# Cosine-similarity attention: a third chunk of exponentials off ScalarE, wide casts of V, late Q sums on TensorE

## The chip, the cores and the metric

The kernel runs on one core of a Trainium2 chip. The core has a matrix engine (TensorE, "PE" in the profile, its weight loads "PEld"), VectorE ("DVE"), ScalarE ("ACT"), GpSimd ("POOL"), SyncE ("SP"), which here issues nearly all transfers, and 16 DMA engines. Each engine works through its own list of instructions in order and waits on semaphores for the others. TensorE writes to PSUM, from which VectorE and ScalarE read; GpSimd works on SBUF alone. The metric is the time of one execution on the device in microseconds (us); the time of a kernel is the median over its runs.

## The reference

Eight batches of twelve heads, 512 rows of 64 numbers each:

```
Q_norm = Q / (norm(Q, axis=-1) + 1e-10)          # Q, K, V: 8 x 12 x 512 x 64, float32
K_norm = K / (norm(K, axis=-1) + 1e-10)
scores  = einsum('bhqd,bhkd->bhqk', Q_norm, K_norm) / tau          # tau = 0.1
weights = exp(scores - max(scores)); weights /= sum(weights) + 1e-10
out     = einsum('bhqk,bhkd->bhqd', weights, V)
```

The scores lie between -10 and 10, so the kernel leaves out the subtraction of the maximum; it gets the row sums from a column of ones beside V.

## The kernel before

The 96 heads are worked as 48 pairs (s = 0 to 47). Each pair of heads goes through these steps, each of them one or a few "operations" of the program; names in brackets are the keys in the code, lines are those of the profile.

- Loads of Q, K and V by SyncE (LD, LV).
- Squares of Q and K on GpSimd in one instruction (SQ, L337), rounded to bf16.
- Their sums by row. For most K (and for Q of the first pairs), TensorE first adds eight slices of eight columns with eight matmuls against the identity (SSQ, L354, into a spare part of the bank for results), and VectorE reduces the rest (RED, L361, 128x64). Where TensorE takes no part, VectorE reduces all 128x512 squares (RED, L365). `on_pe(s, w)` decides which: `Q_ON_PE`, `BY_VECTOR`.
- An inverse square root for a group of pairs by some small VectorE steps (NEW, L389 to L398).
- Scaling of Q (VectorE) and of K (GpSimd, or VectorE for the pairs in `K_ON_DVE`) by it (SCL, L420).
- Eight transposes on TensorE into one PSUM bank (TR, L426, tile tps) and a copy of that bank by VectorE (EVA, L434, tile qt).
- Scores: for each of four chunks c of 128 keys, two matmuls of 512 columns, one for each head (SCO, L508, tile scps). This is called a score group. scps holds two of them, so a score group waits for the exponential two chunks earlier.
- The exponential of the chunk for both heads in one ScalarE instruction, 128x1024 (EXP, L531, tile et).
- A cast of V to bf16 on GpSimd (VC, L536, tile vb).
- Values: for each head h and each quarter i of the queries four matmuls of 65 columns (PV, L548), 32 in all for a pair, into one result bank for each head (tile ops).
- A reciprocal of the row sums (RCP, L559) and the multiplication by it (NRM, L561) on VectorE, here called the division; then the store by SyncE (ST, L565). The first values of the next pair in a bank wait for the division of the pair before.

For chunk 3 of pairs 37 and 45 (`OFF`) ScalarE takes no part: `poly` makes the exponential from a polynomial. TensorE puts that chunk's scores head by head into the bank of the transposes (SCX, L468), VectorE reads each twice (X, L473 and L475), GpSimd does four steps (Y 0 to 3, L479 and L480) and VectorE two more (Y 4 and 5, L486 and L480). Until VectorE has read the second head's scores, the transposes of the next pair wait.

The last pair ends in three pieces (`PIECES`: head 0; head 1 first half; head 1 second half), each with values (L576), reciprocal (L587), division (L589) and store (L593) of its own, by `last`.

No scheduler runs: `ORDER` is a list written out for each engine, of places in the list of operations, and each engine emits them in that order (negative entries are filler matmuls that keep TensorE busy at the start). `due` values decide nothing but which result bank the sums of which pair go to. `RINGS` gives the number of buffers: for Q and K (and vb), V, squares, scaled Q/K, transposed Q/K, exponentials, results and norms.

## Time and profile before

| | |
|---|---|
| time, median of three runs | 189.43 us (189.35 to 189.87) |
| the profiled execution's own time | 189.84 us |
| its span, from the first to the last instruction | 187.9 us |
| ACT busy | 180.8 us (96%), of it L531 174.3 |
| PE, and PEld, busy | 173.7 us (92%), 108.7 us (58%) |
| DVE busy | 172.3 us (92%) |
| POOL busy | 166.8 us (89%) |
| granted TensorE clock | 1.0 all through |
| DMA | 50.76 MB, 270 GB/s over the span |

Busy time is the union of an engine's instructions. Instructions of VectorE, ScalarE and TensorE overlap at their ends, so an instruction's own duration is longer than its distance to the next: an exponential of 128x1024 lasts 1163 ns in the mean, and the next one ends some 917 ns after it. [...]

Rows of the groups that the change touches, as count, mean duration and shape: L337 on GpSimd 44 x 1893 ns (128x1024); L420 on GpSimd 36 x 1042 ns and on VectorE 58 x 677 ns (128x512); L536 on GpSimd 48, most at 626 ns (128x512); L365 on VectorE 48 x 683 ns; L361 on VectorE 40 x 213 ns; L354 on TensorE 368 matmuls; L473 and L475 on VectorE 4 x 688 and 4 x 684 ns; L479 and L480 on GpSimd 4 x 1044 and 4 x 1892 ns; L486 and L480 on VectorE 2 x 1247 and 2 x 676 ns.

### The profile page before, as it was taken

The numbers are of one execution on the slowest core, as the hardware profiler recorded it, in microseconds if no ns is written. First come the engines' busy times: TensorE is split into PE (matmuls) and PEld (weight loads), VectorE is DVE, ScalarE is ACT, GpSimd is POOL, SyncE is SP. The second block draws the span as 40 slices with busy tenths as digits, with TensorE's granted clock in tenths as the row PEclk, the third lists the DMA queues.
The fourth block names the chain that finished last, engine by engine and source line by source line (L and its number), as shares of the span: only waits on it lengthen the run. The fifth ranks groups of instructions, "written<-read, shape, count | busy, mean of one in ns | idle before, by whom it ended". The sixth has DMA issues, their size and how long they took to land.

```text
span 187.9 us, 6635 instructions
## 1 busy us (share of the span) xinstructions
PE 173.7 (92%) x2694; PEld 108.7 (58%) x2694; DVE 172.3 (92%) x546; ACT 180.8 (96%) x212; POOL 166.8 (89%) x152
## 2 busy tenths in 40 slices
PE   6999999999998999999999999899999989999983
PEld 2655666566665666666666556556645446655552
DVE  2789999999999999999999999999999999988864
ACT  4799999999999999999999999999999999999992
POOL 4797999999999999999999999999999999696600
PEclk9999999999999999999999999999999999999999
DMA  4999999899999988999999999976996551312215
GB/s 148 356 350 349 348 354 331 233 328 370 379 385 375 326 243 264 333 304 297 361 379 381 380 380 301 306 244 198 302 336 194 173 167 59 112 59 76 95 59 169
DMA packets 52446, 50.76 MB, mean 270 GB/s; under 512 B 3136, under 2 KB 52416, under 8 KB 52416
## 3 DMA queue, kind: packets, MB, share of 16 engines
q1 hardware_dynamic: 51984, 50.02, 81.1%
q8 instruction: 21, 0.34, 0.8%
q10 hardware_dynamic: 432, 0.33, 0.5%
q14 instruction: 9, 0.07, 0.1%
HBM read 37.75 MB, written 12.58 MB: 268 GB/s over the span
## 4 chain that ended last, share of the span: by engine, by line
ACT 92%; PE 4%; DMA 1%; DVE 1%; issue 1%; POOL 0%
ACT et L531 90%; DMA qk<-in_Q_dram 1%; PE ops L548 1%; PE scps L508 1%; DVE xs L245 0%; PE ops L576 0%; ACT ys L379 0%; DVE ob L589 0%; PE scps L268 0%; POOL qn L258 0%; ACT nps L382 0%; PE tps L268 0%; ACT sq L239 0%; ACT et L522 0%; PE scps L194 0%
## 5 line engine op out<-in xcount | busy, mean ns | idle before, releaser
L531 ACT ACTIVATE et<-scps 128x1024 bf16<-128x1024 f32 (+1 forms) x191 | 174.3, 1151 | 0.5 <-PE scps L508 0.5
L337 POOL TENSOR_TENSOR sq<-qk 128x1024 bf16<-128x1024 f32 x44 | 82.7, 1893 | 1.4 <-DMA qk<-in_K_dram 1.2
L508 PE MATMUL scps<-qt 64*128 64x512 bf16 x380 | 75.2, 386 | 7.8 <-ACT et L531 4.4
L548 PE MATMUL ops<-vb,et 128*128 128x65 bf16 x1504 | 71.6, 194 | 1.1 <-DVE qn L420 0.5
L548 PEld LDWEIGHTS ops<-vb,et 128*128 128x128 bf16 x1504 | 55.1, 98 | 27.1 <-issue 17.4
L420 POOL TENSOR_TENSOR qn<-qk,rk 128x512 bf16<-128x512 f32 x36 | 37.2, 1042 | 2.8 <-DVE rk L394 2.5
L561 DVE TENSOR_TENSOR ob<-ops,rd 128x256 f32<-128x256 f32 x94 | 38.9, 417 | 0.4
L420 DVE TENSOR_TENSOR qn<-qk,nps 128x512 bf16<-128x512 f32 x58 | 38.5, 677 | 0.4 <-ACT nps L382 0.4
L434 DVE COPY qt<-tps 128x1024 bf16<-128x1024 bf16 x47 | 32.3, 687 | 2.6 <-PE tps L426 2.1
L426 PE MATMUL tps<-ident,qn 128*128 128x128 bf16 x376 | 33.9, 221 | 0.1
L508 PEld LDWEIGHTS scps<-qt 64*128 64x128 bf16 x380 | 18.9, 92 | 26.0 <-ACT et L531 11.8
L365 DVE TENSOR_REDUCE nps<-sq 128x8 f32<-128x512 bf16 x48 | 32.3, 683 | 0.0
L536 POOL TENSOR_SCALAR vb<-vf 128x512 bf16<-128x512 f32 x48 | 30.8, 655 | 0.2
L426 PEld LDWEIGHTS tps<-ident,qn 128*128 128x128 bf16 x376 | 21.4, 98 | 12.9 <-issue 6.6
L559 DVE RECIPROCAL rd<-ops 128x4 f32<-128x4 f32 x94 | 16.2, 176 | 3.3 <-PE ops L548 2.3
L354 PE MATMUL ops<-sq,ident 128*128 128x64 bf16 x368 | 18.5, 194 | 0.0
L354 PEld LDWEIGHTS ops<-sq,ident 128*128 128x128 bf16 x368 | 13.9, 98 | 4.1 <-issue 2.7
L361 DVE TENSOR_REDUCE nps<-ops 128x8 f32<-128x64 f32 x40 | 8.5, 213 | 0.6 <-PE ops L354 0.5
L389 DVE TENSOR_TENSOR nps<-nps,ys 128x32 f32<-128x32 f32 (+1 forms) x30 | 6.3, 209 | 0.1
L390 DVE SCALAR_TENSOR_TENSOR nps<-nps,ys 128x32 f32<-128x32 f32 (+1 forms) x30 | 6.2, 208 | 0.1
L480 POOL TENSOR_TENSOR xz<-xz 128x1024 f32<-128x1024 f32 x2 | 3.8, 1892 | 1.5 <-DVE xz L475 1.5
L191 PE MATMUL ops<-warm_in,ident 128*128 128x512 bf16 x8 | 3.6, 628 | 1.4 <-POOL ident L181 1.4
(61 smaller groups left out, 65.0 us busy)
## 6 DMA issues: line engine op xcount, KB each, us to landing
vf<-in_V_dram SPq DMA_DIRECT2D x48, 256.0 KB, 5.8
qk<-in_Q_dram SPq DMA_DIRECT2D x47, 256.0 KB, 5.0
qk<-in_K_dram SPq DMA_DIRECT2D x47, 256.0 KB, 5.7
out_dram<-ob SPq DMA_DIRECT2D x47, 256.0 KB, 3.9
qk<-in_Q_dram SPq DMA_DIRECT2D x2, 128.0 KB, 2.7
qk<-in_K_dram ACTq DMA_DIRECT2D x2, 128.0 KB, 2.9
out_dram<-ob SPq DMA_DIRECT2D x1, 128.0 KB, 1.7
out_dram<-ob ACTq DMA_DIRECT2D x1, 64.0 KB, 1.6
```

Of the source, the lines that this page charges most:

```text
L337: lambda e: e.tensor_tensor(out=sqf, in0=data, in1=data, op=ALU.mult))
L354: last = e.matmul(out=o_ps[bank][:, 320:384], lhsT=ident[:, :], rhs=sq[iqs][:, 8 * w : 8 * w + 8, 8 * k : 8 * k + 8], start=(k == 0), stop ...
L365: lambda e, w=w, dst=dst: e.tensor_reduce(out=dst, in_=sq[iqs][:, 8 * w : 8 * w + 8, :], axis=AX.X, op=ALU.add))
L420: lambda e, w=w, r=r: e.tensor_tensor(out=qn[iqn][:, w].rearrange("p t h d -> p h t d"), in0=qk[iq][:, w].rearrange("p h (t d) -> p h t d" ...
L426: last = e.transpose(t_ps[:, w, t, :], qn[iqn][:, w, t].rearrange("p h d -> p (h d)"), ident[:, :])
L434: lambda e: e.tensor_copy(out=qt[iqt][:, :, :, :].rearrange("p w t x -> p (w t x)"), in_=t_ps[:, :, :, :].rearrange("p w t x -> p (w t x)")))
L508: last = e.matmul(out=sc_ps[:, 2 * b + h, :], lhsT=qt[iqt][64 * h : 64 * h + 64, 1, c, :], rhs=qt[iqt][64 * h : 64 * h + 64, 0, :, :], sta ...
L531: lambda e, c=c, b=b, hs=hs: e.activation(out=et[iet][:, c, hs[0] : hs[-1] + 1, :], in_=sc_ps[:, 2 * b + hs[0] : 2 * b + hs[-1] + 1, :], f ...
L536: lambda e: e.tensor_scalar(out=vb[:, iq, :, :, 0:DIM].rearrange("p c h d -> p h c d"), in0=vf[iv][:, :, :].rearrange("p h (c d) -> p h c ...
L548: last = e.matmul(out=o_ps[h][:, 65 * t : 65 * t + 65], lhsT=et[iet][:, c, h, 128 * t : 128 * t + 128], rhs=vb[:, iq, c, h, :], start=(c = ...
L559: lambda e, h=h, grid=grid: e.reciprocal(out=rd[io][:, h, :], in_=grid[:, :, DIM]))
L561: lambda e, h=h, grid=grid: e.tensor_tensor(out=ob[io][:, h], in0=grid[:, :, 0:DIM], in1=rd[io][:, h, :].unsqueeze(2).to_broadcast([128, N ...
```

## The change

- `OFF` gets chunk 3 of pair 31; ScalarE has 186 exponentials of 128x1024 in its list instead of 187.
- V is cast for two pairs in one instruction of 128x1024 (`JOINT` with "v", from pairs 8 and 9 on; 20 wide casts and 8 narrow ones for 48 narrow ones). The arrays of Q/K, V and vb become one tensor each, and vb's order of heads and chunks is swapped, so that two pairs lie in one access.
- `Q_ON_PE` holds pairs 24 to 46, so that their Q squares are summed first by TensorE.
- `K_ON_DVE` gets pairs 23, 24, 26, 28, 30 and 32.
- Pairs 45, 37 and 31 (`BY_CHUNK`) run their values chunk by chunk, with the polynomial's chunk last, instead of query quarter by query quarter. `LATER` lets the values of pairs 37 and 31 take their turn in the result banks a pair later.
- `RINGS`: 16 buffers for Q and K instead of 15, 6 for scaled Q/K instead of 4, 6 for results instead of 8.
- `ORDER` is another list on every engine. Branches for joint scaling and joint division are there, but `JOINT` names none of them.

```diff
+    def join(self, name, members, eng, kind, due, needs, emit, *rest):
+
+        op = self.add((name, members[-1]) + rest, eng, kind, due, needs, emit)
+        for s in members[:-1]:
+            self.ops[(name, s) + rest] = op
...
-    vb = sb("vb", [128, R_QK, NT, 2, DIM + 1], bf16)
+    vb = sb("vb", [128, R_QK, 2, NT, DIM + 1], bf16)
...
-    for s, w in sorted(((s, w) for s in range(NP) for w in range(2) if on_pe(s, w)), key=lambda j: (due_red(j[0]), j)):
+    for s, w in sorted(((s, w) for s in range(NP) for w in range(2) if on_pe(s, w)), key=lambda j: (j[0] >= EARLY and not j[1], due_red(j[0]), j)):
...
-    for s in range(NP):
+    for s in sorted(range(NP), key=lambda i: i + (1.5 if i in LATER else 0)):
         for h in range(2):
             bank_free[s, h] = before[h]
...
-        P.add(("VC", s), "pool", "vc", T0 + 3.0 - slack(s, M_VC), [("LV", s), key("PV", s - R_QK, 0, NT - 1), key("PV", s - R_QK, 1, NT - 1), "vone"],
-              lambda e: e.tensor_scalar(
-                  out=vb[:, iq, :, :, 0:DIM].rearrange("p c h d -> p h c d"),
-                  in0=vf[iv][:, :, :].rearrange("p h (c d) -> p h c d", c=NT),
-                  scalar1=1.0, scalar2=1.0, op0=ALU.mult, op1=ALU.mult))
+        both = [s - 1, s] if (s, "v") in JOINT else [s]
+        if (s + 1, "v") not in JOINT:
+            P.join("VC", both, "pool", "vc2" if len(both) > 1 else "vc", T0 + 3.0 - slack(s, M_VC),
+                   [("LV", i) for i in both] + [key("PV", i - R_QK, h, NT - 1) for i in both for h in range(2)] + ["vone"],
+                   lambda e: e.tensor_scalar(
+                       out=vb[:, iq + 1 - len(both) : iq + 1, :, :, 0:DIM].rearrange("p r h c d -> p (r h c) d"),
+                       in0=vf[:, iv + 1 - len(both) : iv + 1].rearrange("p r h (c d) -> p (r h c) d", c=NT),
+                       scalar1=1.0, scalar2=1.0, op0=ALU.mult, op1=ALU.mult))
...
                     for c in range(NT):
                         t = i
+                        if s in BY_CHUNK:
+                            t, c = c, last_chunk[i]
                         last = e.matmul(
                             out=o_ps[h][:, 65 * t : 65 * t + 65],
-                            lhsT=et[iet][:, c, h, 128 * t : 128 * t + 128], rhs=vb[:, iq, c, h, :],
-                            start=(c == 0), stop=(c == NT - 1))
+                            lhsT=et[iet][:, c, h, 128 * t : 128 * t + 128], rhs=vb[:, iq, h, c, :],
+                            start=(i == 0 and t == 0) if s in BY_CHUNK else c == 0,
+                            stop=(i == NT - 1) if s in BY_CHUNK else c == NT - 1, skip_group_check=s in BY_CHUNK)
                     return last

-                need, due = sum((exps(s, c) for c in range(NT)), []), T0 + PERIOD + 0.9 * PV_AT[4 * h + i] + late(s)
+                last_chunk = [c for c in range(NT) if c != off_of.get(s)] + [off_of.get(s)]
+                need, due = exps(s, last_chunk[i]) if s in BY_CHUNK else sum((exps(s, c) for c in range(NT)), []), T0 + PERIOD + 0.9 * PV_AT[4 * h + i] + late(s)
...
-OFF = {(45, 3): ((45, 45), False), (37, 3): ((37, 37), False)}
+OFF = {(37, 3): ((37, 37), False), (45, 3): ((45, 45), False), (31, 3): ((31, 31), False)}
...
+LATER = (37, 31)
+BY_CHUNK = (45, 37, 31)
+JOINT = ((11, 'v'), (13, 'v'), (15, 'v'),
...
 BY_VECTOR = (35, 39, 43, 47)
-Q_ON_PE = ()
-K_ON_DVE = (1, 2, 3, 4, 9, 15, 21, 27, 33, 39, 40)
+Q_ON_PE = (24, 25, 26, 27, 28, 29, 30, 31, 32, 33, 34, 35, 36, 37, 38, 39, 40, 41, 42, 43, 44, 45, 46)
+K_ON_DVE = (1, 2, 3, 4, 9, 15, 21, 23, 24, 26, 27, 28, 30, 32, 33, 39, 40)
 VLAG = 3
 LATE, LATE_TO = 0.0, 10
-RINGS = 15, 10, 6, 4, 4, 4, 8, 3
+RINGS = 16, 10, 6, 6, 4, 4, 6, 3
```

What the new lists hold at some places, decoded from `ORDER` by the keys above (PV 35.1 x4 is the four value operations, 16 matmuls, of pair 35, head 1; TR 38 is both transposes' operations, eight matmuls; SSQ 42.0 the sums of Q of pair 42; SSQ 42.1 those of K; SCX 37.1 the lone score matmul of head 1):

```
TensorE, what stands behind the score group (pair, chunk)
           before                                    after
(34, 1)    PV 33 x5                                  PV 31 x3, SSQ 38.1, SSQ 38.0
(35, 3)    SCX 37.1                                  PV 34.0 x2, TR 37
(36, 1)    PV 34.1 x1, PV 35.0 x4                    SCX 37.0, PV 34.1 x1
(36, 2)    SSQ 42.1, TR 38 (K), PV 34.1 x1           PV 34.1 x2, SSQ 41.0
(36, 3)    TR 38 (Q)                                 SCX 37.1
(37, 0)    PV 35.1 x3                                PV 35.0 x4, SSQ 42.1
(37, 1)    PV 35.1 x1, TR 39 (Q)                     PV 35.1 x4, TR 38, SSQ 42.0
(37, 2)    TR 39 (K)                                 PV 36.0 x4, SSQ 43.0
(41, 1)    TR 42 (Q)                                 PV 39.0 x4, PV 39.1 x3
(42, 3)    TR 45, PV 41.0 x2                         TR 44, PV 40 x4
(45, 2)    TR 47                                     PV 43.1 x2, PV 44.0 x3, TR 47 (Q)
(47, 2)    PV 46.1 x3, PV 46.0 x4                    PV 46.1 x4
(47, 3)    piece 1 with half of piece 2, piece 0,     PV 46.0 x4, then pieces 1, 2 and 0,
           the other half of piece 2                 each whole

VectorE at the end (piece k of pair 47 is 47.k)
before     RCP 46.1, NRM 46.1, RCP 46.0, NRM 46.0, RCP 47.1, NRM 47.1, RCP 47.0, NRM 47.0, RCP 47.2, NRM 47.2
after      RCP 46.1, NRM 46.1, RCP 46.0, RCP 47.1, NRM 47.1, NRM 46.0, RCP 47.2, NRM 47.2, RCP 47.0, NRM 47.0
```

On SyncE the loads of pairs 34 to 47 and the stores of pairs 20 to 46 stand in another order: stores 21 to 23 and 24 to 26 follow each other between loads, and stores 28 to 46 stand behind the last load. The two stores of the last pair that SyncE issues stand in the order of pieces 0 and 2, as before.

More of the change, by code (lines that the diff above doesn't have):

```diff
@@ L31, in add, with join2 @@
         return op
+    def join(self, name, members, eng, kind, due, needs, emit, *rest):
+        op = self.add((name, members[-1]) + rest, eng, kind, due, needs, emit)
+        for s in members[:-1]:
+            self.ops[(name, s) + rest] = op
+    def join2(self, name, s, kind, due, needs, emit):
+        self.ops[name, s, 0] = self.add((name, s, 1), "dve", kind, due, needs, emit)
     def schedule(self):
@@ L150, in bass_cosine_similarity_attention_kernel @@
     sc_ps = nc.alloc_psum_tensor("scps", [128, 4, SEQ], f32)
-    o_ps = [nc.alloc_psum_tensor(f"ops{b}", [128, 512], f32) for b in range(2)]
+    o_all = nc.alloc_psum_tensor("ops", [128, 2, 512], f32)
+    o_ps = [o_all[:, b] for b in range(2)]
     t_ps = nc.alloc_psum_tensor("tps", [128, 2, NT, 128], bf16)
@@ L563, in rest @@
                       in1=rd[io][:, h, :].unsqueeze(2).to_broadcast([128, NT, DIM]), op=ALU.mult))
+        if (s, "e") in JOINT:
+            grid = o_all[:, :, 0 : 65 * NT].rearrange("p b (t x) -> p b t x", x=65)
+            due = T0 + PERIOD + 0.9 * PV_AT[7] + late(s)
+            P.join2("RCP", s, "rcp2", due, [x for h in range(2) for x in [("PV", s, h, NT - 1), ("SSQ",) + attached[s, h] if (s, h) in attached else None, key("NRM", s - R_O, h)]],
+                    lambda e, grid=grid: e.reciprocal(out=rd[io][:, :, :], in_=grid[:, :, :, DIM]))
+            P.join2("NRM", s, "nrm2", due + 0.2, [("RCP", s, 1), key("ST", s - R_O)],
+                    lambda e, grid=grid: e.tensor_tensor(
+                        out=ob[io][:, :], in0=grid[:, :, :, 0:DIM],
+                        in1=rd[io][:, :, :].unsqueeze(3).to_broadcast([128, 2, NT, DIM]), op=ALU.mult))
         P.add(("ST", s), "sp", "ld", s + STORE_AT, [("NRM", s, i) for i in range(2)],
```

38 lines of the change are left out of this document (27 added, 11 removed), and 150 rows, old and new, of the table ORDER.

## The prediction

> **What bounds the kernel now.** I read the engine shares first, then the chain of work that ended last.
>
> ```profile
> PE 173.7 (92%) x2694; PEld 108.7 (58%) x2694; DVE 172.3 (92%) x546; ACT 180.8 (96%) x212; POOL 166.8 (89%) x152
> ```
>
> The page's shares: ScalarE is the fullest. And the end of the chain, as start, length and what:
>
> ```profile
> 15.22 149.65 ACT et L531 x163
> 164.86 0.01 issue
> 164.87 14.78 ACT et L531 x16
> 179.65 0.14 issue
> ```
>
> ScalarE's exponentials are the chain from 8.3 us to the end. One chunk (128x1024, L531) costs 149.65 / 163 = 0.918 us of it. Taken singly, the ends of the exponentials lie 0.917 us apart (the median), and only three lie further: 0.974, 1.015 and 1.032 us, ending at 115.21, 161.16 and 165.89. So ScalarE waited 0.06 + 0.10 + 0.12 = 0.27 us there, and 0.14 us ahead of its last pieces. What made it wait shows in TensorE's timeline around the second:
>
> ```profile
> 158.58 0.39 PE L508 MATMUL scps<-qt 64*128 64x512 bf16 x2
> 158.90 0.42 PE L548 MATMUL ops<-vb,et 128*128 128x65 bf16 x8
> 159.16 0.40 PE L354 MATMUL ops<-sq,ident 128*128 128x64 bf16 x8
> 159.39 0.39 PE L426 MATMUL tps<-ident,qn 128*128 128x128 bf16 x4
> 159.71 0.39 PE L508 MATMUL scps<-qt 64*128 64x512 bf16 x2
> 160.03 0.40 PE L426 MATMUL tps<-ident,qn 128*128 128x128 bf16 x4
> 160.36 0.39 PE L508 MATMUL scps<-qt 64*128 64x512 bf16 x2
> ```
>
> The scores of a chunk (L508 x2) need one of two PSUM buffers, so TensorE has one score group to issue per 0.917 us and fits everything else between two of them. Start to start, the rows give 0.32 us for a score group, 0.23 for eight sum matmuls (159.16 to 159.39), 0.26 for eight value matmuls (0.030 each in longer runs), and 0.32 for four transposes and the change to scores, of which 0.22 are the transposes and 0.10 the change. A score group so costs 0.41 and leaves 0.50 us a slot. The slot from 158.58 to 159.71 held 8 values, 8 sums and 4 transposes, 0.70 us: 0.20 too many on top of 0.2 carried in, and ScalarE waited 0.10 us. A score group may start about 0.33 us late before ScalarE notices: those that began 0.43 and 0.44 us late cost it 0.10 and 0.12, one at 0.39 cost 0.06, one at 0.36 at most 0.03. The same counting, slot by slot through the whole old instruction list, gives the lateness of late score groups in the trace to within 0.03 to 0.13 us, mostly too little, except where TensorE itself stood waiting.
>
> **The parts of the change.** *One exponential less:* 0.92 us off the chain.
>
> *VectorE:* six more K scalings (L420, 0.677 each) +4.1; 23 reductions of 128x512 (0.683) become reductions of TensorE's sums (0.213), -10.8; the third chunk's steps, four at 0.686 (L473, L475), 1.247 (L486), 0.676 (L480) and small ones 0.3, +5.0. Sum -1.7. Summed in queue order, the work ahead of the copy L434 that a pair's scores wait for is 1 to 5.5 us less from pair 22 on, but for pairs 36, 37 and 39 (+1.9, +1.0, -0.1), whose copies ended 5.5, 6.6 and 2.7 us early, and before that at most 0.5 more (pair 17, 0.8 early). Nothing on the path, and nothing gained: ScalarE hides it.
>
> *GpSimd:* six K scalings (1.042) -6.3; the third chunk, two at 1.892 and two at 1.044, +5.9; twenty casts of 128x1024 for forty of 128x512 (0.626). The wide cast is in no row: between 0.63 (all of it fixed cost) and 1.25 (two narrow ones). I take 1.04, the one-input 128x1024 of L479, the same operation; -4.2. Sum -4.6, between -13 and -0.4 at the ends. Added in queue order, each square, K scaling and cast ends at least 1.5 us ahead of TensorE's need and, from pair 24 on, 3.3; the old list's leads by the same sum are 1.5 and 3.5, and it kept up. Nothing on the path, at either end. At 148.8 us three casts took 3.19 us where rows give 1.8, beside the off-chunk's L486 and L480 on VectorE; a third chunk stretches GpSimd by 1.4 us once more, inside that lead; were the lead gone, 1.4 us would reach the end. [...]
>
> *SyncE:* stores stand later (20 to 26 in blocks between loads, 28 on behind the last load) and the output ring shrinks from 8 to 6, so the division L561 of pair s waits for store s-6. The last load waits for the cast of pair 37, in GpSimd's sum at 116 to 119 us; store 28 must land for pair 34 at about 140. Nothing, with 20 us of cover; after that each us counts whole.
>
> *TensorE:* 23 times 8 more sum matmuls at 0.029 us: +5.3; one score pair (0.41) out, two lone ones (0.23 each) in. Values by chunk (L548) are as many as before; put a pair later, those of pairs 31 and 37 leave their chunk's chain (two reads 2 us, GpSimd 6.2, VectorE 2.0) some 2 and 3 us to spare, and without that the exponentials four pairs on, which reuse the buffer, would wait it out. This lies between score groups, so slots count, not the sum (slot 34.1 is what stands behind the score group of pair 34, chunk 1). In the new list these pass 0.50 us, and cost, once the free 0.33 is used up: 34.1 (12 values and 16 sums, 0.83) costs 0.18; 35.2 and 35.3 (0.69 each) 0.04; 37.0, 37.1 and 37.2 (0.72, 1.16, 0.72) 0.75; 41.1 and 41.2 (0.85, 0.58) 0.24; 42.3 (0.93) 0.10; 45.2 and 46.0 (0.83, 0.60) 0.10. Sum 1.4 us. The old list counts 0.02 by this and lost 0.27, so I add 0.2 and take 1.6; ends 0.7 (pair 37 alone) and 2.5.
>
> The worst place has a second cause. The scores of pair 37's fourth chunk pass through the transposes' bank, so the transposes of pair 38 wait for VectorE to read it; they stood three slots behind the second such matmul (35.3 to 36.2) and now stand two (36.3 to 37.1), with 16 value matmuls ahead and 8 sums and score group 37.2 queued behind. From X37's first read to the copy of pair 38 the VectorE queue holds 5.4 us (start to start: 0.60 a read, 0.31 a division, 0.60 a scaling, 0.10 to 0.13 small ones), so scores 38.0 come 0.7 to 0.9 us late: the same delay as the count, not a second one.
>
> *The end:*
>
> ```profile
> 183.41 0.42 DVE L561 TENSOR_TENSOR ob<-ops,rd 128x256 f32<-128x256 f32 x1
> 183.45 1.15 ACT L522 ACTIVATE et<-scps 128x256 bf16<-128x256 f32 x3
> ...
> 183.89 0.78 PE L576 MATMUL ops<-vb,et 128*128 128x65 bf16 x18
> ...
> 184.93 0.42 DVE L589 TENSOR_TENSOR ob<-ops,rd 128x256 f32<-128x256 f32 x1
> 185.38 0.82 SPq L593 DMA_DIRECT2D out_dram<-ob  x2
> 185.47 0.29 DVE L589 TENSOR_TENSOR ob<-tps,rd 128x128 f32<-128x128 f32 x1
> ```
>
> The last exponential ends at E = 184.60 and the span 3.3 us later. Before, pair 46's divisions (183.41) were done early. In the new list pair 46's values of head 0 come after the last scores, and their division after that of piece 1, which needs the first of the three last exponentials (ends at E-0.77): matmuls to E-0.50, reciprocal, division to E+0.01, then pair 46's to E+0.35. Only then may the 16 values of piece 0 write that bank: issued and drained by E+1.05 (16 x 0.030 + 0.17), reciprocal and division to E+1.72, where it was E+0.75. Two stores follow, the second issued 0.41 after the first and landed 2.1 later (185.80 to 187.9): E+4.26. So +0.96 us, between 0.3 (should the two orders overlap better) and 1.3.
>
> **Sum.** Span 187.9 - 0.92 - 0.27 - 0.14 + 1.6 + 0.96 = 189.1, that is +1.2. The profiled execution took 189.84 (1.9 outside the span), 0.4 over the runs' median; on 189.43 this is 190.7.
>
> **Rivals.** *The gain holds:* late score groups are made up and the end is not longer: 189.43 - 0.92 - 0.14 = 188.4. For it: GpSimd and VectorE are relieved, PEld is busy 58%. Against it: slot 37.1 alone needs 1.57 us between two scores of 0.92. [...]
> *Late slots, but no longer end:* 189.43 + 0.27 = 189.7.
> *VectorE late at a bank:* each off-chunk (31, 37, 45) holds the transposes' bank as at 38, and VectorE comes late to all: 0.4 more at each, 1.2 in all, 191.9. It decides once the reads start 0.4 us behind the score.
> That the chunk would not leave ScalarE is excluded: its list has 186 whole chunks for 187.
>
> **Numbers.** My forecast 0.54 (190.7, its own range 189.9 to 191.5), gain holds 0.17, no longer end 0.16, bank 0.13. A measurement of this kernel tells 0.3%, 0.57 us, from no change: the first rival is faster; 189.7 lies within, as does the forecast's lowest edge; so 0.17 faster, 0.17 same, 0.66 slower. The range 188.4 to 191.8 leaves out half of the first rival and some of the last.
>
> **What would show it.** Exponentials 0.917 apart except near score groups 34.2, 37.2, 38.0, 41.2 and 43.0, with 0.7 us lost around 38.0; 1.5 us between the scores 37.1 and 37.2; piece 0's division last, 1.7 us after the last exponential. Wrong if these groups follow at 0.92, or if ScalarE waits before pair 20, where the lists hardly differ.

## The result, and the profile after

The changed kernel takes 195.66 us (median of five runs, 195.34 to 196.06), the kernel before 189.5 beside it: 1.0316 times as long, 95% interval 1.0294 to 1.0339. The direction was forecast, the size was not: 6.2 us slower, where the prediction had 1.2, and outside its range. Two runs below, `e8_reordered` and `e9_before_reordered`, had executions at a lower clock that took over 1.5% longer than the fastest; they are left out of the times and ratios. The profiled execution has a span of 193.9 us for 187.9. Its first part on the page:

```profile
PE 179.8 (93%) x2878; PEld 115.9 (60%) x2878; DVE 174.5 (90%) x560; ACT 182.2 (94%) x211; POOL 165.0 (85%) x130
```

ScalarE still has the largest share, but its share fell: it waits. The chain of work that ended last (start, length, what) shows where:

```profile
38.19 34.03 ACT et L555 x37
72.65 0.61 PE ops L577 x16
...
131.50 1.00 DVE et L510
132.50 1.73 issue
...
182.88 2.87 ACT et L555 x3
```

Before, one line of 149.65 us of exponentials ran from 15 to 165 us. Now its longest piece of exponentials runs from 38 to 72 us; from there to the end the chain is a string of short pieces, most of them of TensorE and VectorE. (Lines have moved: exponentials are L555, scores L532, values L577, transposes L450, sums L367, the copy L458, reciprocal and division L592 and L594, squares L350, the casts L563; the off-chunk's closing steps are L510 and L504; the last pair's own values, reciprocals and divisions are L618, L629 and L631.)

The ends of the exponentials, one by one, give the account. Undisturbed they lie 0.917 us apart; what goes beyond that is called a stall here, and summed by pairs (gaps longer by more than 0.02 us):

| us | pairs 2-19 | 20-33 | 34-35 | 36-38 | 39-42 | 43-47 | all | last exponential ends | from there to the end |
|---|---|---|---|---|---|---|---|---|---|
| before | 0.00 | 0.11 | 0.00 | 0.00 | 0.25 | 0.00 | 0.36 | 184.60 | 3.34 |
| after | 0.42 | 1.43 | 1.92 | 1.16 | 0.96 | 0.73 | 6.62 | 189.53 | 4.37 |

So: one exponential less, -0.92; the end, +1.03; stalls, +6.26. The sum, 6.4, is 0.4 above the difference of the spans: pair 4's first exponential ended 0.19 us earlier, and the first piece of the last chunk now ends 0.28 us after the exponential before it, where it was 0.53. The largest stalls are 34.0 (the exponential of pair 34, chunk 0) with 1.56 us, 37.2 with 0.64, 7.3 with 0.35, 34.2 and 41.2 with 0.33, 36.0 with 0.27, 38.0 with 0.26; some twenty more have 0.07 to 0.23.

The slot behind score group 37.1, which the prediction had put first, in TensorE's timeline:

```profile
148.61 0.39 PE L532 MATMUL scps<-qt 64*128 64x512 bf16 x2
148.93 0.69 PE L577 MATMUL ops<-vb,et 128*128 128x65 bf16 x16
149.46 0.61 PE L450 MATMUL tps<-ident,qn 128*128 128x128 bf16 x8
149.90 0.40 PE L367 MATMUL ops<-sq,ident 128*128 128x64 bf16 x8
150.23 0.39 PE L532 MATMUL scps<-qt 64*128 64x512 bf16 x2
```

From one score group to the next it is 1.62 us. Sixteen value matmuls take 149.46 - 148.93 = 0.53 us, 0.033 each; the prediction had 0.030.

And the largest stall, which it had put at nothing, in the timelines of the four engines (in square brackets: idle time before, and who ended it):

```profile
131.33 7.03 POOL L350 TENSOR_TENSOR sq<-qk 128x1024 bf16<-128x1024 f32 x3 [0.59 <-DVE nps L374]
131.42 2.88 DVE L510 SCALAR_TENSOR_TENSOR et<-xz,xw 128x1024 bf16<-128x1024 f32 x1
133.53 0.39 PE L532 MATMUL scps<-qt 64*128 64x512 bf16 x2
134.23 0.17 DVE L592 RECIPROCAL rd<-ops 128x4 f32<-128x4 f32 x1
134.32 0.65 DVE L458 COPY qt<-tps 128x1024 bf16<-128x1024 bf16 x1
134.90 0.41 DVE L594 TENSOR_TENSOR ob<-ops,rd 128x256 f32<-128x256 f32 x1
135.36 0.29 PE L577 MATMUL ops<-vb,et 128*128 128x65 bf16 x4 [1.44 <-DVE ob L594]
136.14 0.39 PE L532 MATMUL scps<-qt 64*128 64x512 bf16 x2
136.57 1.94 ACT L555 ACTIVATE et<-scps 128x1024 bf16<-128x1024 f32 x2 [1.45 <-PE scps L532]
```

L510, the third chunk's step with two SBUF inputs, took 2.88 us where the same step took 1.25 before. Three squares on GpSimd that began with it took 7.03 us where three take 5.6. Behind L510 VectorE's queue held a reciprocal of pair 32, the copy for pair 34 and a division of pair 32, in this order; behind that division stood the first values of pair 31 on TensorE, which need the bank; behind those the score group 34.0, which needs the copy too; behind that ScalarE. This is also the piece of 1.73 us that the chain calls "issue" after L510.

The end is as it was forecast. VectorE's timeline there:

```profile
189.50 0.41 DVE L594 TENSOR_TENSOR ob<-ops,rd 128x256 f32<-128x256 f32 x1
189.86 0.17 DVE L629 RECIPROCAL rd<-tps 128x2 f32<-128x2 f32 x1
...
190.89 0.42 DVE L631 TENSOR_TENSOR ob<-ops,rd 128x256 f32<-128x256 f32 x1
```

Pair 46's division runs as the last exponential ends (189.53); piece 0's comes last and is done at 191.31, 1.78 us after that end (1.7 forecast).

### The profile page after: what moved, and what is told of

It reads as the page before. It is cut to its first block, busy times and chain, and to the rows that moved or that the text cites. A ratio compares the mean times of both kernels' runs of the same rounds, so it can differ in the third digit from the quotient of the medians.

```text
span 193.9 us, 7018 instructions
## 1 busy us (share of the span) xinstructions
PE 179.8 (93%) x2878; PEld 115.9 (60%) x2878; DVE 174.5 (90%) x560; ACT 182.2 (94%) x211; POOL 165.0 (85%) x130
## 4 chain that ended last, share of the span: by engine, by line
PE 36%; DVE 22%; ACT 20%; POOL 8%; DMA 5%; SPq 4%; issue 4%; POOLq 0%
ACT et L555 20%; PE ops L577 13%; PE scps L532 12%; PE tps L450 6%; DMA qk<-in_K_dram 5%; POOL sq L350 4%; DVE ob L594 4%; PE ops L367 4%; DVE qt L458 3%; SPq L324 3%; DVE qn L444 3%; POOL qn L444 2%; DVE nps L374 2%; POOL vb L563 1%; DVE xp L497 1%
## 5 line engine op out<-in xcount | busy, mean ns | idle before, releaser
L555 ACT ACTIVATE et<-scps 128x1024 bf16<-128x1024 f32 (+1 forms) x190 | 175.8, 1055 | 3.8 <-PE scps L532 2.8
L350 POOL TENSOR_TENSOR sq<-qk 128x1024 bf16<-128x1024 f32 x44 | 84.5, 1935 | 2.0 <-DMA qk<-in_K_dram 1.3
L577 PE MATMUL ops<-vb,et 128*128 128x65 bf16 x1504 | 77.6, 195 | 2.6 <-DVE ob L594 1.8
L532 PE MATMUL scps<-qt 64*128 64x512 bf16 x378 | 74.3, 386 | 4.2 <-ACT et L555 1.7
L577 PEld LDWEIGHTS ops<-vb,et 128*128 128x128 bf16 x1504 | 58.1, 98 | 32.5 <-issue 21.5
L444 DVE TENSOR_TENSOR qn<-qk,nps 128x512 bf16<-128x512 f32 x64 | 41.9, 676 | 0.4 <-ACT nps L395 0.4
L594 DVE TENSOR_TENSOR ob<-ops,rd 128x256 f32<-128x256 f32 x94 | 38.9, 417 | 0.4
L444 POOL TENSOR_TENSOR qn<-qk,rk 128x512 bf16<-128x512 f32 x30 | 32.0, 1075 | 5.6 <-DVE rk L407 5.3
L458 DVE COPY qt<-tps 128x1024 bf16<-128x1024 bf16 x47 | 32.1, 683 | 2.9 <-PE tps L450 2.8
L450 PE MATMUL tps<-ident,qn 128*128 128x128 bf16 x376 | 33.4, 220 | 1.3 <-POOL qn L444 0.6
L532 PEld LDWEIGHTS scps<-qt 64*128 64x128 bf16 x378 | 18.4, 92 | 19.6 <-ACT et L555 5.5
L450 PEld LDWEIGHTS tps<-ident,qn 128*128 128x128 bf16 x376 | 21.6, 98 | 10.9 <-issue 3.2
L367 PE MATMUL ops<-sq,ident 128*128 128x64 bf16 x552 | 27.2, 193 | 0.2 <-ACT nps L265 0.2
L563 POOL TENSOR_SCALAR vb<-vf 128x1024 bf16<-128x1024 f32 (+1 forms) x28 | 25.7, 924 | 0.3
L367 PEld LDWEIGHTS ops<-sq,ident 128*128 128x128 bf16 x552 | 20.6, 98 | 5.5 <-issue 3.8
L592 DVE RECIPROCAL rd<-ops 128x4 f32<-128x4 f32 x94 | 16.0, 173 | 5.0 <-PE ops L577 2.7
L378 DVE TENSOR_REDUCE nps<-sq 128x8 f32<-128x512 bf16 x25 | 16.9, 680 | 0.0
L374 DVE TENSOR_REDUCE nps<-ops 128x8 f32<-128x64 f32 x63 | 13.5, 215 | 1.6 <-PE ops L367 1.1
L504 POOL TENSOR_TENSOR xz<-xz 128x1024 f32<-128x1024 f32 x3 | 5.7, 1893 | 5.3 <-DVE xz L499 4.9
L504 POOL TENSOR_TENSOR xw<-xw 128x1024 f32<-128x1024 f32 x3 | 5.7, 1893 | 0.3
```

The lines of the kernel that those rows point to most:

```text
L350: lambda e: e.tensor_tensor(out=sqf, in0=data, in1=data, op=ALU.mult))
L367: last = e.matmul(out=o_ps[bank][:, 320:384], lhsT=ident[:, :], rhs=sq[iqs][:, 8 * w : 8 * w + 8, 8 * k : 8 * k + 8], start=(k == 0), stop ...
L374: lambda e, bank=bank, dst=dst: e.tensor_reduce(out=dst, in_=o_ps[bank][:, 320:384].rearrange("p (g e) -> p g e", e=8), axis=AX.X, op=ALU. ...
L378: lambda e, w=w, dst=dst: e.tensor_reduce(out=dst, in_=sq[iqs][:, 8 * w : 8 * w + 8, :], axis=AX.X, op=ALU.add))
L444: lambda e, w=w, r=r: e.tensor_tensor(out=qn[iqn][:, w].rearrange("p t h d -> p h t d"), in0=qk[iq][:, w].rearrange("p h (t d) -> p h t d" ...
L450: last = e.transpose(t_ps[:, w, t, :], qn[iqn][:, w, t].rearrange("p h d -> p (h d)"), ident[:, :])
```

## The experiments

Two theories stood after the comparison. The first: TensorE is full from pair 20 on, and VectorE's two-input steps lose time to GpSimd. The second kept the prediction's account, that only a few crowded slots and the end cost time, and looked for the rest in single causes: the third chunk, the sums, the bank. The table at the end of this section has the stalls of all runs but `m_port`, in their profiled executions. Times of kernels in one comparison are against the kernel before run beside them (189.6 to 190.1).

**The disputed cost by itself.** `m_port` runs bursts on VectorE and GpSimd side by side.

```diff
+phases = [(stt, 4, none, 0), (none, 0, square, 4), ..., (stt, 4, square, 4), (stt, 4, mulf, 4),
+          (stt, 4, scaleg, 4), (stt, 4, cast, 4), (mul16, 6, square, 4), ..., (scale, 6, square, 4),
+          (copy, 6, square, 4), (redu, 6, square, 4), ...]
```

> No attention is computed here: VectorE and GpSimd run short bursts side by side, started together, and each form's mean time is read. Theory (the two engines hold each other up when both read two SBUF operands): VectorE's 128x1024 step with two f32 SBUF inputs takes 1.25 us alone and beside one-input casts (at most 1.35), and 2 us or more beside GpSimd's two-input squares, as the 2.88 us of pair 31's step; the bf16 product likewise grows from 0.68 by at least half; the scaling and the copy from PSUM and the one-input reduction keep 0.68 within 0.05. Rival A (VectorE never loses, as the prediction priced it): the step stays below 1.4 us beside everything, and only GpSimd's instructions grow. Rival B (any GpSimd work slows any VectorE work): the copy and the reduction grow by a third or more too.

Busy time of L33, the step of L510's form, in five stretches: alone, and beside squares, products of two tensors, scalings of 128x512, and one-input casts.

```profile
5.87:10.60 4.73, 4.63 (x4) 1.00 0.00 0
26.48:37.95 11.47, 9.72 (x4) 1.00 0.00 0
38.00:51.30 13.30, 11.10 (x4) 1.00 0.00 0
51.40:59.40 8.00, 7.10 (x4) 1.00 0.00 0
59.50:67.50 8.00, 7.08 (x4) 1.00 0.00 0
```

And of L48, GpSimd's squares: alone, beside the f32 step, beside the bf16 product (L504's form), beside a scaling with its second operand in PSUM.

```profile
10.58:18.02 7.44, 7.44 (x4) 1.00 0.00 0
26.59:37.95 11.36, 11.36 (x4) 1.00 0.00 0
71.31:80.10 8.79, 8.78 (x4) 1.00 0.00 0
100.13:107.60 7.47, 7.44 (x4) 1.00 0.00 0
```

The columns are the stretch, its length, the engine's busy time and number of instructions, the clock and the DMAs. Alone, four steps take 4.63 us and four squares 7.44; together 11.36, nearly the sum of both (12.07): one after the other, 2.87 us a pair, of which a square's start-to-start time is 1.85 and the step's share 1.0. Singly, a step took 1.22 us alone, 2.92 beside squares, 3.4 beside products of two f32 tensors, 2.06 beside scalings and beside one-input casts; the bf16 product 0.68, 2.38, 1.53 and 1.52. The scaling from PSUM, the copy from PSUM and the reduction of one SBUF operand stayed at 0.68 beside squares, and the squares at 1.89. So the theory's half on casts was wrong (2.06, not at most 1.35), rival A is out, and so is rival B. What was measured reads as turn-taking, each waiting until the other engine's instruction in flight is over: both of VectorE's forms with two SBUF inputs took longer beside each kind of GpSimd's that they were run with here. Beside squares, scalings and casts the addition was GpSimd's own start-to-start time less an overlap of 0.15 or 0.16 (2.92 for 1.22 + 1.85, 2.06 for 1.22 + 1.0, 2.38 for 0.68 + 1.85, 1.53 and 1.52 for 0.68 + 1.0); the product of two f32 tensors was run beside the step only, and has no time alone to set against it. GpSimd's instructions grew too: beside the step four squares took 11.36 us for 7.44, four scalings 8.0 for 4.04, four casts 7.9 for 4.07.

**The third chunk left out.**

```diff
-OFF = {(37, 3): ((37, 37), False), (45, 3): ((45, 45), False), (31, 3): ((31, 31), False)}
+OFF = {(37, 3): ((37, 37), False), (45, 3): ((45, 45), False)}
```

> The changed kernel with pair 31's fourth chunk left on ScalarE and everything else of the change. Theory (the chunk gains 0.92 us of exponentials and pays it back with the 1.56 us stall at 34.0 and its two lone scores): 34.0 has no stall, and the time is 0.1 to 0.6 us below the changed kernel, 195.0 to 195.6, so the other parts account for five sixths of the loss against before. Rival 1 (the third chunk is the main cause): 192.5 or less. Rival 2 (the chunk does what it is for): 196.3 or more.

194.60 us, ratio 1.025 (1.0232 to 1.0268): 1.1 us under the changed kernel, more than expected. 34.0 has no stall, 30.3 and 33.1 (0.20 and 0.15) have gone too, and 36 to 47 are unchanged to 0.01. Set against the other kernel's time, the chunk so costs 1.1 us net where it was to save 0.92, and the other parts make 4.7 us of the whole. Rival 1 is out as the main cause.

**Other work beside the step.** Two trials, with GpSimd's order changed:

```diff
 GpSimd, e2_casts
-(pair 31: Y 3), squares 43, squares 40, squares 45, cast 39, ..., cast 45
+(pair 31: Y 3), cast 39, cast 45, squares 43, squares 40, squares 45, ...
 GpSimd, e5_casts41
+(pair 31: Y 3), cast 39, cast 41, squares 43, squares 40, squares 45, ...
```

> The changed kernel with two of GpSimd's wide casts (39 and 45) moved ahead of its squares 43, 40 and 45, so that VectorE's closing steps of pair 31 run beside one-input work. Theory (the squares stretch the step, and a division that TensorE needs waits behind it): the step L510 of pair 31 takes at most 1.5 us for 2.88, the exponential of score group 34.0 loses its 1.56 us but for at most 0.2, and some 0.3 comes back later because the squares end later: 194.3 to 194.7. Rival (TensorE would have been late at 34.0 anyway, by 12 values, 16 sums and the bank): the stall stays above 1 us and the time above 195.2.

196.58 us, 1.0351 (1.0325 to 1.0377): a miss, and of my own making. L510 took 1.51 us and 34.0 fell to 0.19, as expected. But cast 45 stood 3.3 us on GpSimd for its V, which landed at 134.5 us; the squares behind it came late, VectorE's reduction of squares 43 with them, and 35.0 and 35.1 stalled by 2.58 and 0.60. A part of that has a cause of its own, seen in TensorE's timeline and in the stretch after the pause:

```profile
136.41 0.65 PE L532 MATMUL scps<-qt 64*128 64x512 bf16 x4
139.19 1.06 PE L577 MATMUL ops<-vb,et 128*128 128x65 bf16 x16 [2.12 <-DVE ob L594]
```

```profile
139.00:142.60 3.60, 3.41 (x44) 2.44 (x44) 2.87 (x15) 1.02 (x1) 3.43 (x4) 0.53 0.25 80
```

After the pause of 2.12 us the granted clock (third figure from the end) was 0.53 in the mean of these 3.6 us, and 1.00 in the 3 us before and the 3.4 us after them; the sixteen values took 0.87 us, where sixteen took 0.53 in the changed kernel. The fall is not what made the miss: by itself it lowers the mean clock of a span by 0.009, the other three executions had 0.996 to 0.997 for this one's 0.988, and they still took 196.01 to 196.68 us for 197.21.

> The changed kernel with the wide casts 39 and 41 (whose V lies in SBUF by then) moved ahead of GpSimd's squares 43, 40 and 45. Theory (a VectorE step with two SBUF inputs waits until GpSimd's instruction in flight ends, so 1.0 us at most beside casts and 1.9 beside squares): L510 of pair 31 takes at most 1.6 us for 2.88, score group 34.0 loses all but 0.25 of its 1.56 us, and 35.0 is not late by more than 0.4 since no cast waits for its load: 194.0 to 194.7. Rival (the stall was set by TensorE and returns elsewhere, as in the earlier trial): 195.4 or more.

195.54 us, 1.0295 (1.0269 to 1.0321): 34.0 fell from 1.56 to 0.20, L510 to 1.52. Yet the time fell by 0.4 us only, by the ratios, against an expectation of 1 to 1.6; the intervals of the two ratios overlap. 34.2 and 35.0 took 0.4 back, since pair 31's second closing step (L504) now met the squares, 1.84 us for 0.68; and 41.0 lost 0.69, where nothing had been lost:

```profile
131.15 1.52 DVE L510 SCALAR_TENSOR_TENSOR et<-xz,xw 128x1024 bf16<-128x1024 f32 x1
...
159.17 2.37 DVE L504 TENSOR_TENSOR et<-et,xp 128x1024 bf16<-128x1024 bf16 x1
161.46 0.68 DVE L458 COPY qt<-tps 128x1024 bf16<-128x1024 bf16 x1
```

Cast 41, now at pair 31, had stood ahead of the squares here, and in the changed kernel this step of pair 37 took 1.65 us; now the squares came earlier (3.74 us for two from 157.25), the step waited for nearly a whole one, and the copy for pair 41 stood behind it. The mechanism held both times, and both times the loss came back elsewhere: in `e2_casts` behind a cast that waited for its V, here where such a step next met a long GpSimd instruction. The rival (195.4 or more) gave the time, but not for its reason: TensorE did not set it.

**TensorE's load.** `e6_short_sums` takes matmuls away from the changed kernel (in the order of e5_casts41); `e7_twice` adds as many to the kernel before.

```diff
 e6_short_sums
-                    for k in range(8):
+                    n = 8 if w or s < EARLY else 1
+                    for k in range(n):
...
-                            start=(k == 0), stop=(k == 7))
+                            start=(k == 0), stop=(k == n - 1))
 e7_twice (on the kernel before)
-                    for k in range(8):
+                    n = 16 if s >= 24 else 8
+                    for k in range(n):
...
-rhs=sq[iqs][:, 8 * w : 8 * w + 8, 8 * k : 8 * k + 8],
+rhs=sq[iqs][:, 8 * w : 8 * w + 8, 8 * (k % 8) : 8 * (k % 8) + 8],
```

> The kernel of e5_casts41 with each of the 23 sums for Q on TensorE cut to one matmul of eight (the sums are then partial; all other instructions stay): TensorE has 23 x 7 x 0.029 = 4.7 us less. Theory (TensorE's slots are full from pair 20 to 37, and the many stalls of 0.1 to 0.2 us are its overruns): of the 1.3 us of stalls between pairs 20 and 33 at most 0.4 stays, and 0.5 us or more goes from pairs 36 to 38. After that VectorE's steps of pair 37 meet GpSimd at other moments, so up to 1.2 us may come back at 40.0: 192.3 to 193.8. Rival (the stalls come from VectorE's and GpSimd's queues, not from TensorE's work): no stall before pair 33 changes by more than 0.05, and the time stays within 0.3 us of e5_casts41.

194.38 us, 1.0231 (1.0215 to 1.0248), 1.2 us under e5_casts41. The stalls of pairs 20 to 33 fell from 1.39 to 0.40, those of 36 to 38 from 1.17 to 0.69. Elsewhere little was gained (41.0 still lost 0.48), and the time came out 0.6 above the expected range.

> The kernel before with one thing added: TensorE's sums for K of pairs 24 to 46 take 16 matmuls for 8 (each operand twice, so those sums are doubled). There are 20 such sums, 20 x 8 x 0.029 = 4.6 us, about what the change adds to TensorE with its 23 sums for Q; VectorE, GpSimd and the DMAs have nothing more to do. Theory (this load alone makes the small stalls): 2.2 to 3.2 us slower than before, in stalls of 0.1 to 0.5 us between pairs 24 and 42, about 192.5. The prediction's way of counting (values at 0.030 us, 0.33 us free) gives 1.2 at most, about 191. Rival (TensorE, 58% busy with weight loads, takes it unseen): within 0.3 us of before.

192.07 us, 1.011 (1.0093 to 1.0127), 2.1 us above the kernel before, a little under the expected 2.2 to 3.2. Nothing but TensorE was touched, and there are 1.70 us of stalls between pairs 20 and 33, as in the changed kernel (1.43). The slot behind 28.1, in TensorE's timeline of the kernel before and of this one:

```profile
112.61 0.39 PE L508 MATMUL scps<-qt 64*128 64x512 bf16 x2
112.93 0.66 PE L548 MATMUL ops<-vb,et 128*128 128x65 bf16 x16
113.42 0.40 PE L354 MATMUL ops<-sq,ident 128*128 128x64 bf16 x8
113.75 0.39 PE L508 MATMUL scps<-qt 64*128 64x512 bf16 x2
```

```profile
113.28 0.39 PE L509 MATMUL scps<-qt 64*128 64x512 bf16 x2
113.60 0.66 PE L549 MATMUL ops<-vb,et 128*128 128x65 bf16 x16
114.09 0.63 PE L355 MATMUL ops<-sq,ident 128*128 128x64 bf16 x16
114.65 0.39 PE L509 MATMUL scps<-qt 64*128 64x512 bf16 x2
```

1.14 us has become 1.37, and the exponential 28.2 stalls by 0.42. The rival that judges by the weight loads (58% busy) is out.

**The sums back on VectorE.**

```diff
-Q_ON_PE = (24, 25, 26, 27, ..., 45, 46)
+Q_ON_PE = ()
```

> The changed kernel with the 23 sums for Q back on VectorE (reductions of 128x512, 0.68 us for 0.21) and everything else of the change. Theory (VectorE was as full as TensorE, so the sums have to go somewhere): VectorE has 10.8 us more to do in the 100 us in which it has the third chunk and the six scalings too, its copies and divisions come late at almost every pair, and the time is 199 or more. Rival (the sums on TensorE are what costs): 193 or less.

203.56 us in a single run, so without an interval, with 14.3 us of stalls, as expected (199 or more). In the order as it is, VectorE cannot take them back.

**The order at the end as before.**

```diff
 TensorE
-scores 47.2, values 46 of head 1, scores 47.3, values 46 of head 0, values 47
+scores 47.2, values 46 of head 1, values 46 of head 0, scores 47.3, values 47
 VectorE
-reciprocal 46.0, reciprocal and division of piece 1, division 46.0
+reciprocal 46.0, division 46.0, reciprocal and division of piece 1
```

> The changed kernel with the order at the end as before: pair 46's values of head 0 ahead of the last scores, their division ahead of the last pair's. Prediction's step (the new order at the end costs 0.96 us, 1.07 in the trace): about 194.7, the last store 3.3 us after the last exponential. Rival (pair 45's values now come so late that the bank is not free, and what the end gains the last exponentials lose): the distance shrinks by 0.3 to 0.7 us, the last exponential comes about as much later, and the time stays within 0.3 us of the changed kernel's, 195.4 to 195.9.

195.85 us, 1.0315 (1.0285 to 1.0345): no gain. The way from the last exponential to the end shrank from 4.37 to 4.06, but the last exponential now ends 3.24 us after that of 47.0 instead of 2.88, since the last scores wait behind pair 46's values. The size of the end's cost was right, but it is no matter of those two orders alone: in the old one pair 46's 32 value matmuls start at 187.47 us, when pair 45's division has ended (187.41), and the last scores stand behind them.

**The whole order.** Is it the change's work that is too much, or its order? Four runs reorder the queues of both kernels, by `ORDER` alone, and leave every instruction as it is; two more also give sums back to VectorE (`Q_ON_PE`).

> The changed kernel's own instructions, each as it is, in another order on TensorE (248 of 753 groups moved), VectorE (187 of 560) and GpSimd (37 of 126); the order was chosen by adding up the measured start-to-start times of the traces so far, queue by queue, with the rule that VectorE's two-input steps and GpSimd's instructions take turns. Theory (the change's work fits beside 186 exponentials; its order on the queues does not): hardly a stall over 0.2 us stays but for some 0.5 at 33.2, the last exponential ends near 184.6, the end takes 3.4, and the time is 189.2 to 190.6, as before and 5 to 6 us under the changed kernel. Rival (23 more sums on TensorE from pair 24 on, with 0.50 to 0.58 us of work for a slot of 0.50, cannot be placed): 192.5 or more.

1.0132 (1.0086 to 1.0178) with a wide spread, 190.84 to 193.51 us; the profiled execution took 191.3. Neither side: stalls fell from 6.62 to 3.07, but 9.0 and 9.3 lost 1.06 us and squares 12 and 14 had started on the landing of their loads (37.99 and 42.04 us), which the new order had put off.

> The kernel before, each instruction as it is, reordered by the same procedure (263 of 729 groups on TensorE moved). It tells whether the order of the kernel before leaves anything, so that the gain of the reordered change is not put down to the procedure alone: its stalls are 0.36 us in all, so at most 0.3 to 0.8 us faster than before, 188.9 to 189.7, and no slower than 0.3 us above it.

194.8 us, 1.027 (1.024 to 1.0301), a miss: the same procedure made the kernel before 5 us slower, with four squares between 91 and 136 us waiting for loads, 3.2 us together (stalls 5.13).

> The changed kernel's own instructions reordered again, now with what e8_reordered showed taken into account: its squares 12 to 14 stood waiting for their loads, which GpSimd's and VectorE's new order had made late, so a load counts as landing 4 to 5.5 us after its buffer is free and the order on SyncE's queue is chosen too (279 of 753 groups on TensorE moved, 201 of 560 on VectorE, 38 of 126 on GpSimd, 100 of 193 transfers). Theory (the change's work fits beside 186 exponentials, only its order does not): no wait for a load after pair 6, stalls of 1.5 us at most in all, the end 3.5 us after the last exponential: 188.6 to 190.0, about as before, 5.7 to 7 us under the changed kernel. Rival (the late loads were not the cause, the sums cannot be placed): 192 or more, with stalls between pairs 20 and 33.

190.59 us, 1.0055 (1.0032 to 1.0078). After 20 us no instruction waits for a load any more. 5.1 of the 6.2 us have come back with nothing taken out of the change; the end takes 3.46 again. The time is 0.6 above the expected range all the same: 2.16 us of stalls stay, more than the expected 1.5, 0.92 of them between pairs 20 and 33 (33.2, beside the third chunk's steps, has 0.50).

> The kernel before, reordered with the same rule for loads (269 of 729 groups on TensorE, 199 of 546 on VectorE, 54 of 148 on GpSimd and 103 of 193 transfers moved). Theory (e9_before_reordered was slow because its squares waited for loads): 188.6 to 189.8, at most 0.9 us under the kernel before, with no wait for a load after pair 6. Rival (the procedure itself makes kernels slower, so that the reordered change says nothing of the change): 191.5 or more again. If both land on the same time, the change's content is worth nothing beyond its order: one exponential less is bought with the stalls that remain.

190.0 us, 1.0012 (0.9998 to 1.0026): the procedure finds nothing to gain in the kernel before, and does it no harm once loads are counted. So what it gained on the changed kernel is that kernel's order.

> The reordered change with only 12 of the 23 sums for Q on TensorE (pairs 24, 26 to 46; the other 11 go back to VectorE as reductions of 128x512), in an order chosen in the same way. Theory (what the order could not mend in e10_reordered is TensorE's load: 2.16 us of stalls, 0.9 of them between pairs 20 and 33): TensorE has 11 x 0.232 = 2.6 us less, the stalls fall to 0.8 to 1.6 us and the time to 189.4 to 190.2, as before or a little under. Rival (TensorE's load is no matter any more once the order is mended; VectorE's is): as e10_reordered or slower, 190.5 or more.

193.2 us, 1.0184 (1.0155 to 1.0213), a miss. Between pairs 20 and 33 the stalls fell a little, to 0.76, but 40.2 and 40.3 stalled by 1.92: pair 37's L504 met squares again (1.69 us), TensorE paused for 0.99 us behind a division, and the clock was 0.65 in the mean of the 3.9 us from 157.0 (0.89 in the 3.1 us after them). The profiled execution is the slowest of the six, 194.32 us; the four whose mean clock was 0.999 or 1.0 took 192.78 to 193.45, so the fall of the clock is not what made the miss.

> The same with 8 of the 23 sums on TensorE (pairs 24, 27 to 45). TensorE has 15 x 0.232 = 3.5 us less than in e10_reordered, VectorE 15 x 0.47 = 7 us more. Theory (TensorE's load): as e12_half_sums, 189.2 to 190.2. Rival (VectorE is the next to be full): slower than e12_half_sums by 0.3 us or more.

191.4 us, 1.0087 (1.0063 to 1.011), a miss too: above the theory's range, and faster than `e12_half_sums`. With 8 sums, stalls between pairs 20 and 33 are 1.27, more than with 23 in e10_reordered, and the reductions are VectorE's. So the load cannot just be given back; but the two kernels' orders differ as well, and how much TensorE's load alone makes of the 2.16 us is not settled by them. No version here beats the kernel before.

| stalls, us | 2-19 | 20-33 | 34-35 | 36-38 | 39-42 | 43-47 | all | end after the last exponential |
|---|---|---|---|---|---|---|---|---|
| e1_tail | 0.06 | 1.40 | 1.92 | 1.17 | 0.97 | 0.76 | 6.29 | 4.06 |
| e2_casts | 0.10 | 1.41 | 3.70 | 1.17 | 0.97 | 0.74 | 8.09 | 4.38 |
| e3_nosum | 0.34 | 3.46 | 4.27 | 2.02 | 3.20 | 1.02 | 14.32 | 4.37 |
| e4_nothird | 0.07 | 1.10 | 0.34 | 1.16 | 0.97 | 0.73 | 4.37 | 4.38 |
| e5_casts41 | 0.06 | 1.39 | 0.99 | 1.17 | 1.69 | 0.73 | 6.04 | 4.36 |
| e6_short_sums | 0.06 | 0.40 | 1.11 | 0.69 | 1.78 | 0.92 | 4.96 | 4.39 |
| e7_twice | 0.00 | 1.70 | 0.12 | 0.12 | 0.78 | 0.00 | 2.72 | 3.33 |
| e8_reordered | 1.06 | 0.95 | 0.17 | 0.35 | 0.45 | 0.10 | 3.07 | 3.35 |
| e9_before_reordered | 0.63 | 3.17 | 0.62 | 0.29 | 0.39 | 0.03 | 5.13 | 3.47 |
| e10_reordered | 0.00 | 0.92 | 0.26 | 0.31 | 0.35 | 0.32 | 2.16 | 3.46 |
| e11_before_reordered | 0.10 | 0.28 | 0.00 | 0.00 | 0.25 | 0.18 | 0.81 | 3.47 |
| e12_half_sums | 0.48 | 0.76 | 0.09 | 0.58 | 2.80 | 0.36 | 5.07 | 4.46 |
| e13_third_sums | 0.05 | 1.27 | 0.43 | 0.07 | 0.47 | 0.25 | 2.53 | 3.86 |

## Why the prediction was wrong

Two steps failed. The first is TensorE's term: "Sum 1.4 us. The old list counts 0.02 by this and lost 0.27, so I add 0.2 and take 1.6; ends 0.7 [...] and 2.5." The trace has 6.62 us of stalls, 6.26 more than before and 5.0 more than the 1.6 taken. The places it named did stall, each by more than it said; the term was too small, and it left out other places. The second is VectorE's term, which put the third chunk's step at nothing on the path. It cost 1.56 of the 6.26 us, at 34.0.

*The price of a value matmul.* "0.26 for eight value matmuls (0.030 each in longer runs)": 0.26 / 8 is 0.033, which is what sixteen take in the slot above, and the lower figure was used. In a slot of 12 to 16 values that is 0.04 to 0.05 us, and it adds up where a slot is full. The traces' matmuls between score groups can be counted again in the same way (a sum matmul 0.029 us, a transpose 0.056, a lone score matmul 0.23; the room is 0.917 less 0.41 for the score group, 0.507). With 0.030 for a value the changed kernel counts 1.3 us, with 0.033 it counts 2.2, and 22.2, 25.0 and 33.2 are then among the places, which were not on the list; the kernel before counts 0.1 and 0.5, where 0.36 was lost. By the price of 0.033 TensorE has a mean of 0.51 us of work a slot in pairs 20 to 28 and in 32 to 34, and 0.58 in 35 to 37, for a room of 0.507; the kernel before has 0.46, 0.46 and 0.37. The term was summed over the few slots that stood out; that the mean had reached the limit was not looked at. The windows view shows the same without a count. The kernel before, then after, summed over 74 to 126 us:

```profile
sum 52.00, PE 49.50 PEld 31.69 DVE 51.15 ACT 52.00 POOL 51.33; mean PE 16.50 PEld 10.56 DVE 17.05 ACT 17.33 POOL 17.11
```

```profile
sum 52.00, PE 51.21 PEld 34.06 DVE 47.66 ACT 51.68 POOL 50.19; mean PE 17.07 PEld 11.35 DVE 15.89 ACT 17.23 POOL 16.73
```

VectorE is relieved by 3.5 us where ScalarE hardly waited before (0.11 us of stalls in pairs 20 to 33), and TensorE, which sets the scores, is busy for all but 0.8. e7_twice and e6_short_sums show that this load costs time in the orders given: as much load on the old order costs 2.1 us, and without it 1.0 of the 1.4 us between pairs 20 and 33 goes.

A full mean does not set the loss by itself, though. e10_reordered has the same matmuls and much the same means (0.50, 0.53 and 0.54 in the three stretches), and loses 0.92 us in pairs 20 to 33 and 0.57 in 34 to 38, where the changed kernel loses 1.43 and 3.08. The load leaves little room to make lateness up; the order decides how much lateness there is.

*A step with two SBUF inputs on VectorE.* The prediction priced L486 (now L510) at 1.247 us from rows in which it ran beside the end of a cast (1.298) or beside an idle GpSimd (1.196), saw casts stretched beside it, and put the cost on GpSimd alone: "a third chunk stretches GpSimd by 1.4 us once more, inside that lead". It said of VectorE "Nothing on the path, and nothing gained: ScalarE hides it", and named neither the division behind the step in its queue nor the bank that TensorE gets from it. At 34.0 that cost 1.56 us. m_port shows the turn-taking. e4_nothird and e5_casts41 show that the stall hangs on it: in the latter L510 is 1.36 us shorter, and so is the stall. The prediction did not ask which of the two engines waits.

The rest of the 6.26 us, some 2.5 us by the recount, is probably TensorE's other waits for copies and divisions, which a count of slots leaves out; no run takes it apart. What the runs do show is that most of the loss from pair 34 on, the stall at 34.0 included, goes with the order: e10_reordered has 1.2 us there, where the changed kernel has 4.8.

Point by point:

- *One exponential less, 0.92.* Right; but by e4_nothird the chunk costs 1.1 net, so it gives back some 2.0. The 0.14 us ahead of the last pieces went too, and a little more (0.25).
- *VectorE -1.7.* Its busy time rose by 2.2, mostly since the closing steps hold 3.2 us of waiting (L510 1.23, 1.71 and 2.88, L504 0.69, 0.83 and 1.65).
- *GpSimd, a wide cast at 1.04.* 1.045 measured. Busy time fell by 1.8, not 4.6, with 2.9 us of turns waited for. "At least 1.5 us ahead" was too kind: in the profiled execution the K scaling of pair 8 stood behind the wide cast 11 and came late, and the exponential 7.3 lost 0.35 us; "Wrong [...] if ScalarE waits before pair 20" so holds by the letter. Runs with the same order there (e1_tail, e4_nothird) do not show that stall.
- *SyncE, nothing.* Right: no store or load of the changed kernel is waited for after the first pairs but one of the squares (35), off the path.
- *Slots.* 37.2 and 38.0 lost 0.90 for 0.75 forecast, 34.2 0.33 for 0.18, 41.2 and 41.3 0.43 for 0.24, 43.0 0.22 for 0.10, 45.0 to 46.1 0.38 for 0.10: the places right, each too small. 22.2 to 30.3 and 40.0 to 40.2 were not on the list.
- *The end, 0.96.* 1.03.
- *Rivals.* "VectorE late at a bank" was nearest in kind: a VectorE queue that gives a bank too late. But the bank was that of the results, not that of the transposes, and the price 1.56 at one place. "The gain holds", which had "PEld is busy 58%" in its favour, is refuted by e7_twice: added to the kernel before, whose weight loads are busy 58%, 4.6 us of matmuls (20 x 8 x 0.029) cost 2.1. "Late slots, but no longer end" is out by the end's 1.03.

## What to carry to other kernels

Where one engine must deliver in every slot, first add its whole work over a stretch of slots and divide, with the price per instruction taken from the densest runs of just that kind; when the mean reaches the slot, lateness is no longer made up, and naming the worst slots finds only a part of the loss (here 1.6 of 6.6 us). Then the order of the queues decides: here the same instructions in another order gave 5.1 of 6.2 us back. Work moved from a busy engine to another that is as full is no relief, though its shares look alike (92% and 92% here). In these runs a VectorE instruction with two SBUF inputs had no price of its own beside a working GpSimd (1.22 us alone, 2.92 beside squares): add the longest instruction that GpSimd may have in flight, and look at what stands behind it in VectorE's queue.

## What the runs showed of the hardware

- In m_port VectorE's instructions with two SBUF inputs and GpSimd's took turns: 1.22 us for an f32 step alone, 2.92 beside squares of 1.85, 2.06 beside casts of 1.0; none of it beside squares for a scaling with one operand in PSUM, a copy from PSUM and a reduction of one SBUF operand (0.68 either way).
- TensorE's granted clock fell after short pauses in two runs: to 0.53 in the mean of 139.0 to 142.6 us after one of 2.12 us (e2_casts), to 0.65 in the mean of 157.0 to 160.9 around one of 0.99 that ended at 158.0 (e12_half_sums). After 1.44 us in the changed kernel it stayed at 1.00 (129 to 140 us), so the length of the pause alone did not decide. In e2_casts sixteen values took 0.87 us in that stretch, for 0.53, so the stall there cost a second time.
